# Seven-product matmul with row normalisation: products chained from bank to bank instead of combined on the vector engine

## The chip, the cores and the metric

The kernel runs on one core of one Trainium2 chip. The metric is device time in microseconds (us) of one launch. A core has five engines with a queue of instructions each, executed in the order written: TensorE (PE in the profile, its weight loads PEld), VectorE (DVE), ScalarE (ACT), GpSimd (POOL) and SyncE (SP). The last two mostly issue DMAs here. Matmuls write to PSUM, which has eight banks of 128 x 512 fp32 per core.

## The reference

```python
x = np.matmul(a, b)                                   # a, b: 2048 x 2048, fp32
rms = np.sqrt(np.mean(x ** 2, axis=-1, keepdims=True) + eps)
return (gamma * x / rms).astype(np.float32)
```

## The kernel before

The rows of a are cut into 16 row blocks of 128, the columns of b into four chunks of 512 (`CH`), the inner dimension into 16 tiles of 128, taken in 8 pairs `kp`. Matmuls take 16-bit operands (bf16 or fp16) and accumulate in fp32.

**Seven products.** Two row blocks (a *group* `g`), two column chunks (a *half* `j`: left or right 1024 columns) and the even and odd inner tiles make a 2 x 2 by 2 x 2 block product. The kernel forms its four output quarters x11, x12, x21, x22 (128 x 512 each) from seven products of eight matmuls instead of eight products. Each product has a left side, a quarter of the transposed a or a sum of two of them (`a_sums`, VectorE), and a right side, a quarter of b or a sum of two (`b_sums`, `b_sums_in_place`, VectorE), made once for all groups.

**Stages.** First, row blocks 0 to 3 (the head) are multiplied with the left columns while b arrives: TensorE transposes a, each pair `kp` is transposed through the one bank `tbank` and used at once (`stream`, `stream_in_parts`). Second, the right columns: blocks 0 and 1 plainly (`stream_right`), blocks 2 and 3, the group `PAIR`, with products 2, 5 and 1 as b arrives, and then 4, 3, 7 and 6. Third, the groups 2 to 6, each with two halves (`group_half`), and last group 7 (`last_group`).

**Order.** The schedule is written out by hand: every engine executes its instructions in the order in which the program issues them, and `hooks_of` says between which products the other work (finishing earlier rows, preparing the next a) is issued.

**In a half** (lines 582 to 626), product 2 is copied from its bank by ScalarE (L597), product 5 added to it on VectorE (L601), product 1 minus that gives t (L605). Products 4 and 3 then go on in the banks of 2 and 5 (`start=False`), are copied by ScalarE (L608, L613), squared there (L303, with the sum of squares), and added to t on VectorE (L610, L615); 7 and 6 are added on VectorE (L619, L624). So a half has six vector adds, three copies and four squares of 128 x 512. The next half uses other banks out of the seven of a rotating pool.

**Rows.** The next a is loaded as fp32 (L121, POOL), each row's norm computed on ScalarE (`row_norm`), a power of two `factor` made from it on VectorE (`row_factor`, four operations on 128 x 1), and the row scaled into fp16 (`row_apply`): on VectorE for blocks 4 and 5 (L240), on ScalarE from block 6 on (L242). A transposing DMA issued by SyncE (L195) then writes `at`. The load for the next but one group waits until the fp32 buffer is read, of which there are two. `finish` computes a row block's root (`take_rms`: reduce on VectorE L335, root on ScalarE L337), its reciprocal (L346), multiplies both halves with it and gamma (L370) and stores them (L376, SyncE).

**Last group.** The products of its right half are ordered so that row block 14 is complete early. Its last product of all, 6 of the right half, accumulates in two halves of 256 columns (L800) on banks that VectorE has filled with the rest of the sum; two squares, a root (L352), a reciprocal and the scalings follow.

## Time and profile before

| what | us |
|---|---|
| median of 3 runs | 221.31 |
| lowest, highest | 221.05, 221.69 |
| profiled execution: span from first to last instruction | 219.1 |
| first matmul of the chain's unbroken part to the end of the last matmul | 66.73 to 212.2 |
| mean granted TensorE clock | 0.994 |

The runs carry no separate time for the profiled execution: the median stands 2.2 us above its span (221.31 - 219.1), and that is taken as what lies around it.

In the profile, a row of the groups reads: line, engine, operation, output tile <- input tiles, shapes, count, then busy us, mean ns of one, and idle us before, with what ended it. A row of the order of time reads: start us, length us, what. Rows of waits read: engine, line, what it waited for, us in total, times, longest.

### The profile page before, as it was taken

To read this page: it belongs to the slowest core of one execution; us is meant where nothing else is said; L and a number is where in the kernel's file an instruction comes from. 1 tells how busy PE (TensorE), PEld (TensorE's weight loads), DVE (VectorE), ACT (ScalarE), POOL (GpSimd) and SP (SyncE) were. 2 spreads that over 40 slices of the span, in tenths; PEclk is the share of its full clock that TensorE was granted. 3 is DMA by queue.
4 is the path that set the end of the run, shared out by engine and by line. 5 is a ranking of instruction groups with operands and counts; after the bars stand their busy time and mean duration, and the time that the engine had idled before them with its cause. 6 is when DMAs were issued, how large, how long until landed. Compare 5 with 4: busy or idle time off the path is not lost.

```text
span 219.1 us, 3041 instructions
## 1 busy us (share of the span) xinstructions
PE 209.2 (95%) x1032; PEld 97.7 (45%) x1032; DVE 165.9 (76%) x326; ACT 127.0 (58%) x263; POOL 36.4 (17%) x75
## 2 busy tenths in 40 slices
PE   7799999999999999999999999999999999999970
PEld 3344544444455444444444444444444444444440
DVE  1128899999989998969696639946795759787771
ACT  2110002930599898588945996289747996334471
POOL 7554443433020002200110002000200000000040
PEclk9999999999999999999999999999999999999997
DMA  7999999999929698946799149955699259145045
GB/s 156 168 202 206 204 206 209 212 208 228 407 77 330 243 276 218 349 188 165 212 320 399 64 88 271 350 244 96 160 298 400 37 106 361 79 167 219 1 170 215
DMA packets 36720, 46.60 MB, mean 213 GB/s; under 512 B 22240, under 2 KB 26336, under 8 KB 35424
## 3 DMA queue, kind: packets, MB, share of 16 engines
q0 software_dynamic: 10608, 23.86, 44.1%
q1 hardware_dynamic: 25824, 22.29, 33.7%
q10 hardware_dynamic: 272, 0.26, 0.3%
q8 instruction: 8, 0.13, 0.2%
q14 instruction: 8, 0.07, 0.1%
HBM read 34.60 MB, written 16.78 MB: 234 GB/s over the span
## 4 chain that ended last, share of the span: by engine, by line
PE 92%; DMA 3%; ACT 1%; POOL 1%; issue 1%; DVE 0%; ACTq 0%; POOLq 0%
PE acc L285 71%; PE acc L388 16%; DMA early<-in_a_dram 3%; PE tbank L419 2%; PE tbank L168 2%; PE acc L800 1%; POOL b L102 0%; PE acc L185 0%; PE tbank L185 0%; ACT a L738 0%; DVE head_at L173 0%; ACTq L850 0%; ACT sq L803 0%; ACT rms L352 0%; POOL t_left masks.py:199 0%
## 5 line engine op out<-in xcount | busy, mean ns | idle before, releaser
L285 PE MATMUL acc<-b,s 128*128 128x512 bf16 x408 | 93.3, 379 | 0.0
L285 PEld LDWEIGHTS <-s 128*128 128x128 f16 (+1 forms) x512 | 50.0, 98 | 59.6 <-DVE s L260 0.2
L388 PE MATMUL acc<-b,head_at 128*128 128x512 bf16 x176 | 43.0, 379 | 1.2 <-DMA b<-in_b_dram 0.8
L303 ACT ACTIVATE sq<-x 128x512 bf16<-128x512 f32 x53 | 33.4, 630 | 6.9 <-DVE x L731 3.0
L370 DVE SCALAR_TENSOR_TENSOR x<-x,r,gamma_sb 128x1024 f32<-128x1024 f32 x28 | 34.9, 1282 | 0.7
L219 ACT ACTIVATE sq<-a 128x1024 bf16<-128x1024 f32 x24 | 25.3, 1054 | 3.2 <-DMA a<-in_a_dram 2.5
L388 PEld LDWEIGHTS <-head_at 128*128 128x128 bf16 x176 | 16.9, 97 | 20.4 <-issue 1.3
L242 ACT ACTIVATE head_at<-a,s 128x2048 f16<-128x2048 f32 x10 | 20.0, 1996 | 3.3 <-DVE s L229 3.3
L102 POOL DMA_DIRECT2D b<-in_b_dram x32 | 17.2, 541 | 20.6 <-DMA b<-in_b_dram 14.2
L430 ACT COPY x<-acc 128x512 f32<-128x512 f32 x5 | 2.9, 582 | 24.6 <-PE acc L388 24.6
L285 PEld LDWEIGHTS <-head_at 128*128 128x128 f16 (+1 forms) x112 | 10.9, 98 | 13.2
L285 PE MATMUL acc<-early,head_at 128*128 128x512 bf16 x64 | 14.5, 379 | 0.0
L285 PEld LDWEIGHTS <-at_even 128*128 128x128 f16 x96 | 9.4, 98 | 11.3
L285 PE MATMUL acc<-early,s 128*128 128x512 bf16 x56 | 14.2, 379 | 0.0
L260 DVE TENSOR_TENSOR s<-head_at 128x1024 f16<-128x1024 f16 (+5 forms) x22 | 13.4, 635 | 0.1
L615 DVE TENSOR_TENSOR x<-x,x 128x512 f32<-128x512 f32 x9 | 6.2, 693 | 8.8 <-ACT x L613 8.3
L127 POOL COPY pace<-x 128x1 f32<-128x1 f32 x4 | 1.7, 413 | 66.2 <-DVE x L624 64.9
L597 ACT COPY x<-acc 128x512 f32<-128x512 f32 x9 | 5.2, 573 | 11.5 <-PE acc L285 11.5
L173 DVE COPY head_at<-tbank 128x1024 bf16<-128x1024 bf16 x7 | 4.8, 692 | 8.6 <-PE tbank L168 8.5
L285 PE MATMUL acc<-t_left,s 128*128 128x512 bf16 x48 | 11.3, 379 | 0.0
L783 POOL TENSOR_SCALAR x<-x,r 128x512 f32<-128x512 f32 x1 | 2.7, 2657 | 51.2 <-DVE r L346 51.2
L276 DVE TENSOR_TENSOR b<-b 128x1024 bf16<-128x1024 bf16 x16 | 10.8, 686 | 0.2
(112 smaller groups left out, 238.0 us busy)
## 6 DMA issues: line engine op xcount, KB each, us to landing
out_dram<-x SPq DMA_DIRECT2D x29, 512.0 KB, 3.7
a<-in_a_dram POOLq DMA_DIRECT2D x10, 1024.0 KB, 9.0
b<-in_b_dram POOLq DMA_DIRECT2D x32, 256.0 KB, 10.0
a<-in_a_dram POOLq DMA_DIRECT2D x4, 512.0 KB, 9.8
early<-in_a_dram POOLq DMA_DIRECT2D x7, 256.0 KB, 10.0
gamma_sb<-in_gamma_dram POOLq DMA_DIRECT2D x2, 512.0 KB, 8.4
out_dram<-x SPq DMA_DIRECT2D x3, 256.0 KB, 2.6
out_dram<-a SPq DMA_DIRECT2D x1, 768.0 KB, 3.3
```

The lines of the kernel that those rows point to most:

```text
L102: nc.gpsimd.dma_start(out=raw[j][kp][:, t, :], in_=b[lo:lo + P, j * HALF:(j + 1) * HALF])
L173: nc.vector.tensor_copy(out=head_at[:, 2 * kp:2 * kp + 2, :, :], in_=view)
L219: nc.scalar.activation(out=junk, in_=a32[mb][:, h * HALF:(h + 1) * HALF], func=ACTF.Square, scale=2.0 ** -8, accum_out=n2[:, h:h + 1])
L242: nc.scalar.activation(out=a16[mb], in_=a32.pop(mb), func=ACTF.Copy, scale=factor.pop(mb))
L260: nc.vector.tensor_tensor(out=sum_of(g, s)[:, lo:hi, :], in0=x[:, lo:hi, :], in1=y[:, lo:hi, :], op=op)
L276: nc.vector.tensor_tensor(out=flat[:, 1:3, :], in0=flat[:, 1:3, :], in1=flat[:, 0::3, :], op=ALU.add)
L285: nc.tensor.matmul(bank, lhsT[:, kp, :], rhs, start=(start and kp == 0), stop=(kp == KP - 1), skip_group_check=not start)
L303: nc.scalar.activation(out=sq[:, 0:CH], in_=src, func=ACTF.Square, scale=inv_sqrt_n, accum_out=msq[mb][:, c:c + 1])
L370: nc.vector.scalar_tensor_tensor(out=x, in0=x, scalar=inverse_of[mb], in1=gamma_sb[:, h * HALF:(h + 1) * HALF], op0=ALU.mult, op1=ALU.mult)
L388: nc.tensor.matmul(bank, head_at[:, kt, r, :], head_rhs(c, kt), start=(kt == 0), stop=(kt == KT - 1))
L597: nc.scalar.copy(out=c, in_=one[1])
L615: nc.vector.tensor_tensor(out=t, in0=t, in1=x12, op=ALU.add)
```

## The change

The seven products take another form, in which products accumulate on one another in PSUM:

- P1 = a11 b11. Its bank is copied by ScalarE to a second bank (B1 to B2); P2 = a12 b21 then accumulates in B1, which is x11.
- P6 accumulates on the copy in B2; B2 is copied to a third bank B3. P5 accumulates in B3. P7 has a bank of its own, B7, which ScalarE copies to x21's place.
- x22 = B3 + P7's copy (VectorE). After that P3 accumulates in B3, which is x12, copied by ScalarE. P4 accumulates in B2; x21 = B2 + P7's copy (VectorE).

A half has two adds, five copies (two of them from bank to bank), and the squares run over 1024 columns (`square_half`). a needs the sums 3, 1, 2, 4 (`a_sums`), where 1 overwrites the quarter a21 and 2 is made from 1, 4 from 2; b needs `b_diff` and a chain of three in `b_rest`, the first in place.

The products of neighbouring halves are interleaved (`segment`): P6 of half n, P3 of half n-1, P2 of n, P1 of n+1, then P5, P7 and P4 of n. The hooks are replaced by this written order. All eight banks are named tiles; there is no rotating pool. The pair of the second stage takes the same form: its P1, P2, P7 while b arrives, then P6, P3, P5, P4. Its results are put together in `pair_ends`, issued in segment 0 after row block 0 is finished. Rows are scaled on VectorE for all blocks (`row_apply`). The slots of x are listed per group. In the last group the order is P6, P3 (of the half before), P2, P1, P5, then P6 (right), P3, P2 (right), P5 (right), P7, P3 (right), P7 (right), P4 and P4 (right) in two column halves.

The diff, cut (blank lines and the removed bodies of functions printed above are left out):

```diff
-    ps_t = ctx.enter_context(tc.tile_pool(name="ps_t", bufs=1, space=bass.MemoryType.PSUM))
-    ps_a = ctx.enter_context(tc.tile_pool(name="ps_a", bufs=7, space=bass.MemoryType.PSUM))
+    psum = ctx.enter_context(tc.tile_pool(name="psum", bufs=1, space=bass.MemoryType.PSUM))
...
+    tbank = psum.tile([P, CH], FP32, name="tbank")
+    acc = [psum.tile([P, CH], FP32, name=f"acc_{n}") for n in range(7)]
...
-    s_sum = {s: consts.tile([P, KP, P], FP16, name=f"s_{s}") for s in (1, 2, 5, 6, 7)}
+    s_sum = {s: consts.tile([P, KP, P], FP16, name=f"s_{s}") for s in (2, 3, 4)}
...
     def row_apply(mb):
         a16[mb] = a16_slot(mb)
-        if mb < HB + 2:
-            nc.vector.tensor_scalar_mul(out=a16[mb], in0=a32.pop(mb), scalar1=factor.pop(mb))
-        else:
-            nc.scalar.activation(out=a16[mb], in_=a32.pop(mb), func=ACTF.Copy,
-                                 scale=factor.pop(mb))
+        nc.vector.tensor_scalar_mul(out=a16[mb], in0=a32.pop(mb), scalar1=factor.pop(mb))
+    def prepare(mb):
+        row_factor(mb)
+        row_apply(mb)
+        transpose_dma(mb)
...
+    slot_of = {(r, h): r + HB * h for r in range(HB) for h in range(2)}
+    for n, slots in enumerate(((0, 4, 1, 5), (2, 6, 3, 7), (4, 5, 0, 1), (6, 7, 2, 3),
+                               (5, 1, 4, 0), (7, 3, 6, 2))):
+        for m, slot in enumerate(slots):
+            slot_of[HB + 2 * n + m % 2, m // 2] = slot
...
+    def sum_of(g, s):
+        if s == 1:
+            return quarter(g, 1, 0)
+        return s_sum[s].bitcast(BF16) if g < G0 else s_sum[s]
+    def a_sums(g, which):
+        a11, a12, a21, a22 = (quarter(g, r, c) for r in range(2) for c in range(2))
+        terms = {3: (a11, a21, ALU.subtract), 1: (a21, a22, ALU.add),
+                 2: (sum_of(g, 1), a11, ALU.subtract), 4: (a12, sum_of(g, 2), ALU.subtract)}
+        for s in which:
+            x, y, op = terms[s]
+            nc.vector.tensor_tensor(out=sum_of(g, s), in0=x, in1=y, op=op)
+    def b_quarter(j, kp, r, c):
+        return raw[j][kp][:, r, c * CH:(c + 1) * CH]
+    def b_diff(j, kp):
+        add(sums[j][:, 1, kp, :], b_quarter(j, kp, 1, 1), b_quarter(j, kp, 0, 1), ALU.subtract)
+    def b_rest(j, kp):
+        b11, t1, b21, b22 = (b_quarter(j, kp, r, c) for r in range(2) for c in range(2))
+        t2, t4 = sums[j][:, 0, kp, :], sums[j][:, 2, kp, :]
+        add(t1, t1, b11, ALU.subtract)
+        add(t2, b22, t1, ALU.subtract)
+        add(t4, b21, t2, ALU.subtract)
+    def product_matmul(g, j, m, bank, kp, start):
+        lhsT = {1: lambda: quarter(g, 0, 0), 2: lambda: quarter(g, 0, 1),
+                3: lambda: sum_of(g, 4), 4: lambda: quarter(g, 1, 1), 5: lambda: sum_of(g, 1),
+                6: lambda: sum_of(g, 2), 7: lambda: sum_of(g, 3)}[m]()
+        rhs = {1: lambda: b_quarter(j, kp, 0, 0), 2: lambda: b_quarter(j, kp, 1, 0),
+               3: lambda: b_quarter(j, kp, 1, 1), 4: lambda: sums[j][:, 2, kp, :],
+               5: lambda: b_quarter(j, kp, 0, 1), 6: lambda: sums[j][:, 0, kp, :],
+               7: lambda: sums[j][:, 1, kp, :]}[m]()
+        nc.tensor.matmul(bank, lhsT[:, kp, :], rhs, start=(start and kp == 0),
+                         stop=(kp == KP - 1), skip_group_check=not start)
+    def product(g, j, m, bank, start=True):
+        for kp in range(KP):
+            product_matmul(g, j, m, bank, kp, start)
...
+        if kp == KP - 2:
+            before.append(lambda: a_sums(PAIR, (3,)))
...
+    u2, u4, p7 = acc[4:7]
     def stream_right(kp):
         first, second = ([(g, 2 * kp + t) for g in plain] for t in range(2))
         if kp == 0:
+            for both in zip(first, second):
+                for g, kt in both:
+                    head_matmul(banks[g], *g, kt)
+            product_matmul(PAIR, 1, 1, u2, kp, True)
+            product_matmul(PAIR, 1, 2, u4, kp, True)
             return
+        product_matmul(PAIR, 1, 1, u2, kp, True)
+        for g, kt in first:
+            head_matmul(banks[g], *g, kt)
+        product_matmul(PAIR, 1, 2, u4, kp, True)
+        product_matmul(PAIR, 1, 7, p7, kp - 1, True)
+        for g, kt in second:
+            head_matmul(banks[g], *g, kt)
     for kp in range(KP):
         load_later(1)
+        b_diff(1, kp)
         stream_right(kp)
+        if kp % 2 == 0:
+            square_half(kp // 2, 0)
         if kp > 0:
+            b_rest(1, kp - 1)
         if kp == 0:
+            b_diff(0, KP - 1)
+            b_rest(0, KP - 3)
         if kp == 1:
+            b_rest(0, KP - 2)
+            b_rest(0, KP - 1)
+        if kp in (2, 3, 4):
+            a_sums(PAIR, ((1,), (2,), (4,))[kp - 2])
...
+    copy_on("A")(out=x11, in_=u2)
+    product_matmul(PAIR, 1, 7, p7, KP - 1, True)
+    add(x11, u4, x11)
+    b_rest(1, KP - 1)
+    evict(plain[:2], "DA")
     row_norm(HB)
     row_norm(HB + 1)
+    product(PAIR, 1, 6, u2, start=False)
+    nc.vector.tensor_copy(out=u4, in_=u2)
+    evict(plain[2:3], "D")
     row_factor(HB)
     row_apply(HB)
+    product(PAIR, 1, 3, acc[0])
+    product(PAIR, 1, 5, u4, start=False)
     row_factor(HB + 1)
     row_apply(HB + 1)
+    evict(plain[3:], "A")
+    turned = [transpose_half(HB, 0, tbank)]
+    for kp in range(KP):
+        product_matmul(PAIR, 1, 4, u2, kp, False)
+        if kp == 4:
+            turned.append(transpose_half(HB, 1, acc[1]))
     load_gamma(0)
     load_block(HB + 3)
+    take_transposed(HB, 0, turned[0], nc.scalar.copy)
+    turned += [transpose_half(HB + 1, h, bank) for h, bank in enumerate((tbank, acc[2]))]
+    take_transposed(HB, 1, turned[1], nc.scalar.copy)
+    for h in range(2):
+        take_transposed(HB + 1, h, turned[2 + h], nc.vector.tensor_copy)
+    a_sums(G0, (3, 1, 2))
     def pair_ends():
+        nc.scalar.copy(out=x22, in_=p7)
+        nc.scalar.copy(out=x12, in_=u4)
+        add(x21, u2, x22)
+        add(x22, x12, x22)
+        add(x12, acc[0], x12)
...
+    halves = [(g, j) for g in range(G0, NG) for j in range(2)]
+    B1, B2, B3, B7 = (acc[1], acc[0]), acc[3:5], (acc[6], acc[5]), acc[2]
+    def chunks(n):
+        g, j = halves[n]
+        return [x_chunk(2 * g + r, 2 * j + c) for r in range(2) for c in range(2)]
+    def do(n, m):
+        if n >= len(halves) or n < 0:
+            return
+        g, j = halves[n]
+        b1, b2, b3 = B1[n % 2], B2[n % 2], B3[n % 2]
+        product(g, j, m, {1: b1, 2: b1, 3: b3, 4: b2, 5: b3, 6: b2, 7: B7}[m],
+                start=m in (1, 7))
+        if m == 1:
+            nc.scalar.copy(out=b2, in_=b1)
+        elif m == 6:
+            nc.scalar.copy(out=b3, in_=b2)
+        elif m == 7:
+            nc.scalar.copy(out=chunks(n)[2], in_=B7)
+    def take(n, what, engine="A"):
+        x11, x12, x21, x22 = chunks(n)
+        if what == 11:
+            copy_on(engine)(out=x11, in_=B1[n % 2])
+        elif what == 12:
+            copy_on(engine)(out=x12, in_=B3[n % 2])
+        elif what == 22:
+            add(x22, B3[n % 2], x21)
+        else:
+            add(x21, B2[n % 2], x21)
     def load_after(g, mb):
         wait_for(at(2 * g + 3)[:, KT - 1, 0:1] if g == G0 else x_chunk(2 * g + 1, 1)[:, 0:1])
         load_block(mb)
+    def segment(n):
+        g, j = halves[n]
+        ra, rb, nxt = 2 * g, 2 * g + 1, 2 * g + 2
+        if n == 0:
+            do(n, 1)
+            take_rms(0)
+            finish(0)
+            do(n, 2)
+            pair_ends()
+            a_sums(g, (4,))
+            row_norm(nxt)
+            take_rms(1)
+            do(n, 6)
+            prepare(nxt)
+            finish(1)
+            do(n + 1, 1)
+            row_norm(nxt + 1)
+            do(n, 5)
+            do(n, 7)
+            take(n, 22)
+            take(n, 11)
+            prepare(nxt + 1)
+            do(n, 4)
+            take(n, 21)
+            square_half(rb, j)
+            return
+        if j == 1 and g + 2 < NG:
+            load_after(g, nxt + 2)
+            if g == G0:
+                wait_for(x_tile(r2, 1)[:, 0:1])
+            load_block(nxt + 3)
+        do(n, 6)
         if j == 0:
+            take_rms(ra - 1)
+            if g + 1 < NG:
+                row_norm(nxt)
+        elif g == G0:
+            square_half(r2, 1)
+            square_half(r3, 1)
+        do(n - 1, 3)
+        take(n - 1, 12)
+        square_half(halves[n - 1][0] * 2, 1 - j)
+        if j == 0:
+            a_sums(g, (4,))
+            if g == G0 + 1:
+                take_rms(r3)
+                finish(r3)
+            finish(ra - 1)
+        elif g == G0:
+            take_rms(r2)
+        do(n, 2)
+        take(n, 11)
+        if j == 0:
+            take_rms(ra - 2)
+            if g + 1 < NG:
+                prepare(nxt)
+        elif g == G0:
+            finish(r2)
         else:
+            finish(ra - 2)
+        do(n + 1, 1)
+        if j == 0 and g + 1 < NG:
+            row_norm(nxt + 1)
+        do(n, 5)
+        do(n, 7)
+        take(n, 22)
+        if j == 0 and g + 1 < NG:
+            prepare(nxt + 1)
+        if j == 1 and g + 1 < NG:
+            a_sums(g + 1, (3, 1, 2))
+        do(n, 4)
+        take(n, 21)
+        square_half(rb, j)
     def last_group():
...
+        do(n, 6)
+        take_rms(rb - 2)
+        do(n - 1, 3)
+        take(n - 1, 12)
+        square_half(ra - 2, 1)
+        a_sums(g, (4,))
+        finish(rb - 2)
+        do(n, 2)
+        take(n, 11)
+        do(n + 1, 1)
+        take_rms(ra - 2)
+        do(n, 5)
+        nc.scalar.copy(out=x22[0], in_=b3[0])
+        finish(ra - 2)
+        do(n + 1, 6)
+        do(n, 3)
+        take(n, 12)
+        square_half(ra, 0)
+        do(n + 1, 2)
+        take(n + 1, 11)
+        square_of(ra, x11[1])
+        add(xa, xa, gam_left, ALU.mult)
+        do(n + 1, 5)
+        nc.scalar.copy(out=x22[1], in_=b3[1])
+        pre_a = partial(ra, 2)
+        do(n, 7)
+        add(x22[0], x21[0], x22[0])
+        wide = a_pool.tile([P, K], FP32, name="a32")
+        chunk = [wide[:, c * CH:(c + 1) * CH] for c in range(NCH)]
+        add(chunk[1], x22[0], gam[1], ALU.mult)
+        do(n + 1, 3)
+        take(n + 1, 12)
+        square_of(ra, x12[1])
+        other = B1[0]
+        product(g, 1, 7, other)
+        halves2 = [slice(0, CH // 2), slice(CH // 2, CH)]
+        half = [bank[:, 0:CH // 2] for bank in (B1[1], b3[0])]
+        rms_a = root(msq[ra][:, 3:4], pre_a)
+        nc.scalar.copy(out=x21[1], in_=other)
+        for bank, col in zip(half, halves2):
+            add(bank, b2[1][:, col], x21[1][:, col])
         r_a = inverse(rms_a)
         left, mid = xa[:, 0:CH], xa[:, CH:]
         by_r(left, r_a)
         nc.sync.dma_start(out=rows(ra, 0, CH), in_=left)
         nc.gpsimd.tensor_scalar_mul(out=mid, in0=mid, scalar1=r_a)
         scaled_gamma(x_tile(ra, 1), x_tile(ra, 1), r_a, gamma_sb[:, HALF:])
         nc.sync.dma_start(out=rows(ra, HALF, N), in_=x_tile(ra, 1))
         nc.sync.dma_start(out=rows(ra, CH, HALF), in_=mid)
+        add(x22[1], x21[1], x22[1])
+        square_of(rb, x22[1])
+        do(n, 4)
+        add(x21[0], b2[0], x21[0])
+        square_half(rb, 0)
+        add(xb[:, 0:CH], xb[:, 0:CH], gam[0], ALU.mult)
+        add(chunk[3], x22[1], gam[3], ALU.mult)
+        pre_b = partial(rb, 2)
...
-                nc.tensor.matmul(bank, s_sum[6][:, kp, :], b_quarter(1, kp, 0, 1)[:, col],
+                nc.tensor.matmul(bank, quarter(g, 1, 1)[:, kp, :], sums[1][:, 2, kp, col],
...
-                nc.vector.tensor_scalar(out=part, in0=half_sq[:, 0:1], scalar1=pre_b,
-                                        scalar2=msq[rb][:, 2:3], op0=ALU.add, op1=ALU.add)
-        r_b = inverse_rms(half_sq[:, 1:2], part)
+                add(part, half_sq[:, 0:1], pre_b)
+        r_b = inverse(root(half_sq[:, 1:2], part))
...
+    square_half(0, 1)
+    square_half(1, 1)
+    for n in range(len(halves) - 2):
+        segment(n)
```

## The prediction

> **What bounds the kernel now.** First the page: busy time by engine and the engines' shares of the chain that ended last.

> ```profile
> span 219.1 us, 3041 instructions
> PE 209.2 (95%) x1032; PEld 97.7 (45%) x1032; DVE 165.9 (76%) x326; ACT 127.0 (58%) x263; POOL 36.4 (17%) x75
> PE 92%; DMA 3%; ACT 1%; POOL 1%; issue 1%; DVE 0%; ACTq 0%; POOLq 0%
> ```

> TensorE is the bound; no other engine is near it. Then the chain in order of time (start, length, what):

> ```profile
> 66.73 143.74 PE acc L285 x666
> 210.47 1.76 PE acc L800 x16
> ...
> 212.82 0.30 ACT rms L352
> ```

> From 66.7 us on TensorE never waits: 143.74/666 = 0.216 us per matmul, 1.73 us per product of eight. The root that opens the tail starts 0.6 us after the last matmul. So the change can gain little, and whatever makes TensorE wait lengthens the kernel one for one. A row of TensorE's waits and one of VectorE's order of time show what is already tight:

> ```profile
> PE acc L388 <- DMA b<-in_b_dram: 0.8, 1, 0.8
> 56.53 1.10 DVE L271 TENSOR_TENSOR early<-b 128x512 bf16<-128x512 bf16 x3 [0.32 <-DMA b<-in_b_dram]
> ```

> The first is TensorE's longest wait after its warm-up; the second says that the last quarter of b reaches VectorE only at 56.5. Last, the rows by shape, for prices:

> ```profile
> L260 DVE TENSOR_TENSOR s<-head_at 128x1024 f16<-128x1024 f16 x15 | 9.7, 682 | 0.0
> L601 DVE TENSOR_TENSOR x<-acc,x 128x512 f32<-128x512 f32 x9 | 6.2, 686 | 0.0
> L370 DVE SCALAR_TENSOR_TENSOR x<-x,r,gamma_sb 128x1024 f32<-128x1024 f32 x28 | 34.9, 1282 | 0.7
> L240 DVE TENSOR_SCALAR gamma_sb<-a,s 128x2048 f16<-128x2048 f32 x1 | 1.3, 1277 | 0.0
> L242 ACT ACTIVATE head_at<-a,s 128x2048 f16<-128x2048 f32 x10 | 20.0, 1996 | 3.3 <-DVE s L229 3.3
> L613 ACT COPY x<-acc 128x512 f32<-128x512 f32 x10 | 5.8, 575 | 1.7 <-issue 0.9 <-PE acc L285 0.8
> L310 ACT ACTIVATE sq<-x 128x1024 bf16<-128x1024 f32 x4 | 4.3, 1067 | 0.0
> L147 PE MATMUL acc<-sq 128*128 128x512 bf16 x8 | 3.6, 631 | 1.4 <-DVE pace L137 1.4
> ```

> and two pairs of neighbours on VectorE (start, length):

> ```profile
> 72.81 0.68 DVE L563 TENSOR_TENSOR x<-x 128x512 f32<-128x512 f32 x1
> 73.52 0.69 DVE L564 TENSOR_TENSOR x<-x,x 128x512 f32<-128x512 f32 x1
> ...
> 187.91 0.68 DVE L619 TENSOR_TENSOR x<-acc,x 128x512 f32<-128x512 f32 x1
> 188.51 0.68 DVE L260 TENSOR_TENSOR s<-head_at 128x1024 f16<-128x1024 f16 x1
> ```

> Independent operations start 0.60 apart; one that overwrites what the one before reads starts 0.71 after it.

> **The change, part by part.** "Pn" is product n. A matmul ends 0.16 us after the next could start (0.38 long against 0.216).

> *Engine totals per group of two halves.* VectorE: adds 12 to 4, sums of a 5 to 4, row scaling 0 to 2: -8x0.60 - 0.60 + 2x1.28 = -2.8 us. ScalarE: copies 6 to 10, squares 8 of 128x512 to 4 of 128x1024, row scaling out (2x2.0): about -4 us. Both were off the path: worth 0. TensorE's matmuls are as many as before: 0. Loads are issued in the same order: 0, covered by the stages before, except where named.

> *Chain copies.* P6 accumulates on a copy of P1, P5 and P3 on a copy of P6. In the loop P5, P7 and P4 of the half before (5.2 us) lie between P1 and P6, and three products between P6 and P5, against a copy of 0.58 on ScalarE: 0. ScalarE writing a bank from a bank is in no row; I take its copy from a bank (0.58), with VectorE's 0.70 into a bank as the other end; the difference stays under cover.

> *Group boundaries.* The next group opens with P6, which needs sum 2 of a. VectorE's order is fixed: the add that takes quarter 22 (needs P7's copy), sum 3, sum 1 (in place on what sum 3 reads), sum 2 (from sum 1). Only P4 (1.73) lies on TensorE between P7 and that P6. From P7's nominal end: 0.16 + copy 0.59 + 0.03, add 0.60 to the next start, 0.71, 0.71, last sum 0.68, hand-over and weight load about 0.12: 3.60; less 1.73 = **1.87 us** of waiting. Before, the sum of the opening product was made four products ahead. Behind the sums on VectorE stands the add of quarter 21, behind that ScalarE's square and P6's chain copy, there 2.5 us after P6 starts; P5 wants it at 6.9: 0 more. Groups 2-3 to 6-7 make five: **9.35**. With all starts 0.60 apart it is 1.65 each (8.2).

> *Right columns, last products of the pair.* b_diff and b_rest cost VectorE 0.34 + 0.45 + 0.45 + 0.34 = 1.57 per step (0.42 long, 0.335 apart, 0.45 if dependent) against 1.6 before; it is free again when b's last quarter lands at 56.5. Then: b_diff to 56.87, b_rest(6) to 58.1, the add on x11 to 58.7, b_rest(7) to 59.94, the eviction of acc[0] to 60.63. P6 runs 58.30 to 60.03; P3 writes acc[0] and waits to 60.65: **0.62**. If VectorE were 0.6 earlier it is 0, if b lands later it grows.

> *Opening of group 2 (segment 0).* P1 starts at 67.8 (67.2 before, +0.62). P2 follows it at once and accumulates on the very bank that is being copied: it waits 0.16 + 0.59 + 0.04 = **0.79**. P2 to 72.05, P6 to 73.78. P1 of half 1 writes acc[0], which holds the pair's P3 until the last of pair_ends. VectorE: transposed copies and three sums to 70.8, reduce, ScalarE's root 71.1, reciprocal, finish(0) 71.3 to 73.73 (2x1.20), three adds to 75.73. P1 waits 73.78 to 75.76: **1.98**. The root and the chain copy behind it reach 77.2, in time for P5 at 77.49. Half 1 of group 2 then finds its copies early (86.7 against 89.6): 0.

> *Group 3 (its P6 at 0).* ScalarE: square 0.5-1.7, copy to 2.5, root, row_norm to 5.15, take 12, square to 6.85, root of row block r3 7.05. VectorE stands from 4.45 to 7.05 for that root, then finishes r3 (to 9.67) and block 5 (12.26), and only then reduces block 4, whose root ScalarE awaits at 12.65 ahead of P1's chain copy (13.15). P6 of half 1 could start at 12.08: **1.09**. Behind it row_norm ends 15.6, P7's copy 16.2, the add that frees P3's bank 16.9; P3 could start at 14.90: **2.02**. In later groups there is no r3, and the copy is there at 8.1.

> *Row scaling on VectorE.* 1.28 for 2.0. Its transposing DMA on SP follows it, landing 4.3 after issue: the second of a group is scaled by 13.9 (P6 at 0), landed by 18.3, read at 23.9. The load on POOL that waits for its buffer is issued at 14.2 and lands in 9.0 (5.1 to 12.8), wanted at 34. Stores behind them on SP free buffers wanted half a group later. All 0; each would cost its overrun.

> *Tail.* The last products are now P7, P4 and P4 in two column halves. After P7 the seeds of 256 columns end at 22.24 (last group's P6 at 0), the reciprocal at 22.3, then on VectorE: scaling 1.20, add 0.60, add 0.68 to 24.83; ScalarE squares x of row block b 25.0-26.2 and the two column halves to 27.4; VectorE, which overwrites what that square reads, multiplies, multiplies, sums and adds from 26.1 to 27.75; root at 27.8. The last matmul ends at 24.3: 3.5 us to the root against 0.6: **2.9** (0 if these queues drain earlier, 4 if the seeds are late too).

> *Sum.* 0.62 + 0.79 + 1.98 + 9.35 + 1.09 + 2.02 + 2.9 = 18.75. The profiled span goes from 219.1 to 237.9; the median shown, 221.31, stands 2.2 above the span, and I carry that: **240.1 us**.

> *Clock.* After the 0.8 us wait above, the granted clock reads 1.00 (8 to 10 us and on). From a cold start eight matmuls took 3.60 us against 1.73, so a wait that cools TensorE costs up to 1.87. There are ten waits of 0.6 to 2.0, nearer to the 0.8: 0, at most 18.7. [...]

> *Seeds.* The kernel before already accumulates on a bank that VectorE wrote (L731, then L800's 16 matmuls in 1.76 us), at no extra instruction, so the copies get no further term. [...]

> **The rivals.** *Part of the piles drain earlier (229 to 236).* The boundary stays (8.2 to 9.4), with none to half of the rest (9.4): 221.3 + 8.2 = 229.5 at least, 234.2 with half. For it: VectorE has 2.8 us less to do per group. Against: the waits follow from order, not from load. Chance 0.16.

> *More waits (244 to 254).* In the right columns sum 1 is written in place into head_at at stride two; if that orders TensorE's next reads of head_at behind it, TensorE waits from 46.2 to 48.7, 2.4 more; or some waits cool the clock, at up to 1.87 each. No row shows a strided write beside TensorE's reads, and the page shows a clock of 9 tenths up to the tail. 243 to 252; chance 0.14.

> *The sums are hidden (219 to 223; the other side).* If sums 3, 1, 2 were done by P4's end, the boundary is 0; then the openings must vanish too. It decides if P7's end to sum 2 takes under 1.73 us; copy, add and three sums at their shortest starts are 3.3. Time 221.3 with the tail's 2.9 gone as well. Chance 0.05; faster in 0.03 of it, since nothing shortens TensorE's own work.

> **How the numbers follow.** Forecast, own range 236 to 244: 0.65. About 0.3% (0.7 us) is what this kernel's measurement can tell from no change. The range 232.5 to 247 leaves out the last rival, the lower part of the first and the upper part of the second, together under 0.2. Faster 0.03, same 0.02, slower 0.95.

> **What would show it.** In the profile after: TensorE near 209 busy in a span near 238; its waits led by "VectorE sum of a", five times some 1.9 us, about 26.0 us apart; one wait near 70 on a ScalarE copy and one near 74 on VectorE's pair add; two in group 3; ScalarE's last root 3 to 4 us after the last matmul. Wrong if sum 2 precedes P4's end, if finish(0) isn't ahead of the pair adds, or if the matmul after a wait runs slower than 0.216 apart.

## The result, and the profile after

| what | before | after |
|---|---|---|
| median, lowest to highest (4 runs each, side by side), us | 221.5 (221.05 to 221.78) | 265.87 (263.3 to 268.73) |
| ratio, 95% interval | 1 | 1.192 (1.188 to 1.196) |
| profiled execution / its span, us | not given / 219.1 | 263.89 / 262.1 |
| mean granted TensorE clock | 0.994 | 0.949 |
| first matmul of the groups to the end of the last matmul | 66.73 to 212.2 | 67.67 to 252.06 |

The ratio, and every comparison below, leaves out runs more than 1.5% above the fastest of their kernel, here 267.84 and 268.73; the other two make 263.6 us for the changed kernel. The changed kernel is 19% slower; the forecast was 240.1, with 247 as its upper end. 43.0 us of span have to be found (262.1 - 219.1), against 18.75 forecast.

The page of the changed kernel: span, busy time by engine, the granted clock over the span in 40 slices, and the shares of the chain that ended last:

```profile
span 262.1 us, 2910 instructions
PE 219.9 (84%) x1032; PEld 99.9 (38%) x1032; DVE 143.8 (55%) x278; ACT 114.4 (44%) x227; POOL 39.0 (15%) x71
PEclk9999999999997999999968999799995899999995
DMA 37%; PE 37%; DVE 13%; ACT 4%; issue 4%; POOL 2%; ACTq 0%; DVEq 0%; POOLq 0%; SPq 0%
```

Two things stand here that the forecast did not have. The chain is 37% DMA, as much as TensorE; before it was 3% against 92%. Not all of that is new waiting: 16% are loads of b in the first 56 us, a stage in which the chain of before ran through TensorE, and 16% are transposing DMAs (11 into `at_even`, 5 into `head_at`). And the clock has holes: 7 in the slice at about 80 us, then 6 and 8 near 135, 7 near 168, 5 and 8 near 200 (the last 5 is the tail). TensorE's busy time is 10.7 us more for the same 1032 matmuls.

TensorE's waits in the changed kernel (engine, output, line, what it waited for: us in total, times, longest):

```profile
PE acc L344 <- DVE s L321: 21.5, 5, 7.0
PE acc L344 <- DVE x L98: 4.7, 1, 4.7
PE acc L344 <- DVE s L229: 1.9, 1, 1.9
PE acc L344 <- ACT acc L517: 1.4, 2, 0.8
PE acc L344 <- DVE x L393: 0.6, 1, 0.6
```

These are the ten waits that were forecast, at the places that were forecast; the view has no others after the start of the right columns. (The third row names `s L229`, the first operation of `row_factor`; it stands directly behind the add of quarter 22, for which the wait was forecast.) But the first row was to be 9.35 and the second 1.98. TensorE's order of time shows which of them are longer (start, length, what, and in brackets the idle time ahead and what ended it):

```profile
78.51 5.15 PE L344 MATMUL acc<-b,at_even 128*128 128x512 bf16 x16 [4.68 <-DVE x L98]
...
100.93 1.90 PE L344 MATMUL acc<-t_left,s 128*128 128x512 bf16 x8 [1.73 <-DVE s L321]
...
135.27 3.59 PE L344 MATMUL acc<-t_left,s 128*128 128x512 bf16 x8 [7.00 <-DVE s L321]
138.66 2.40 PE L344 MATMUL acc<-b,s 128*128 128x512 bf16 x8
...
166.26 2.93 PE L344 MATMUL acc<-t_left,s 128*128 128x512 bf16 x8 [4.48 <-DVE s L321]
...
198.82 3.60 PE L344 MATMUL acc<-t_left,s 128*128 128x512 bf16 x8 [6.53 <-DVE s L321]
...
227.69 1.90 PE L344 MATMUL acc<-t_left,s 128*128 128x512 bf16 x8 [1.73 <-DVE s L321]
```

The boundaries into groups 3 and 7 wait 1.73, as worked out (1.87, less the 0.16 by which the shown wait is short, since it counts from the modelled end of the last matmul). Those into groups 4, 5 and 6 wait 7.00, 4.48 and 6.53, and after each the next eight matmuls take 2.9 to 3.6 us instead of 1.9. Only these three lie behind a group in which loads of the next a go out beside the transposing DMA: the loads of group 2 wait for that DMA in the program's text, and group 6 issues none. The chain tells what the three waited for:

```profile
119.66 13.29 DMA at_even<-head_at
133.07 0.70 DVE s L321
133.80 0.70 DVE at_even L321
134.52 0.70 DVE s L321
135.27 12.70 PE acc L344 x48
...
151.34 12.59 DMA head_at<-head_at
...
181.78 14.71 DMA at_even<-head_at
```

The transposing DMA of the group's second row block, issued at 119.66, lands 13.29 us later, and only then can VectorE make sums 3, 1 and 2, behind which the opening product stands. In the kernel before, its kind landed in 4.3 (4.4 at most); that is what the forecast used.

The sum over the trace:

| term | forecast | measured |
|---|---|---|
| pair's P3 behind an eviction | 0.62 | 0.61 + 0.16 |
| P2 behind the copy of P1 (segment 0) | 0.79 | 0.66 + 0.16 |
| P1 of half 1 behind the pair's adds | 1.98 | 4.68 + 0.16 |
| group 3: P6, then P3 | 1.09 + 2.02 | 0.79 + 1.89 + 2 x 0.16 |
| five boundaries | 9.35 | 21.47 + 5 x 0.16 |
| slow matmuls after waits | 0 (to 18.7) | 1.5 + 2.2 + 1.7 + 2.9 = 8.3 |
| tail, end of the last matmul to the end | 2.9 | 10.0 - 6.9 = 3.1 |
| sum | 18.75 | 43.1 |

The slow matmuls are the lengths above and of the eight behind them, against 1.89 per eight (3.62 per sixteen).

### The profile page after: what moved, and what is told of

Its sections match the earlier page's. It is cut to its first block, busy times and chain, and to the rows that moved or that the text cites. A ratio compares the mean times of both kernels' runs of the same rounds, so it can differ in the third digit from the quotient of the medians.

```text
span 262.1 us, 2910 instructions
## 1 busy us (share of the span) xinstructions
PE 219.9 (84%) x1032; PEld 99.9 (38%) x1032; DVE 143.8 (55%) x278; ACT 114.4 (44%) x227; POOL 39.0 (15%) x71
## 4 chain that ended last, share of the span: by engine, by line
DMA 37%; PE 37%; DVE 13%; ACT 4%; issue 4%; POOL 2%; ACTq 0%; DVEq 0%; POOLq 0%; SPq 0%
PE acc L344 37%; DMA b<-in_b_dram 16%; DMA at_even<-head_at 11%; DMA head_at<-head_at 5%; DMA early<-in_a_dram 3%; DVE x L298 3%; DMA gamma_sb<-in_gamma_dram 3%; DVE s L321 3%; DVE x L98 2%; ACT sq L221 2%; POOL b L112 1%; ACT x L521 1%; DVE head_at L321 1%; DVE early L98 1%; POOL a L131 1%
## 5 line engine op out<-in xcount | busy, mean ns | idle before, releaser
L344 PEld LDWEIGHTS <-s 128*128 128x128 f16 (+1 forms) x312 | 31.8, 103 | 68.3 <-DVE s L321 23.9
L267 ACT ACTIVATE sq<-x 128x1024 bf16<-128x1024 f32 (+1 forms) x33 | 33.6, 1018 | 47.7 <-DVE x L98 47.1
L344 PE MATMUL acc<-t_left,s 128*128 128x512 bf16 x96 | 27.1, 434 | 21.5 <-DVE s L321 21.5
L357 PE MATMUL acc<-b,head_at 128*128 128x512 bf16 x176 | 43.2, 379 | 0.1
L344 PE MATMUL acc<-b,head_at 128*128 128x512 bf16 x168 | 40.5, 379 | 0.0
L344 PE MATMUL acc<-b,at_even 128*128 128x512 bf16 x144 | 34.7, 392 | 5.3 <-DVE x L98 4.7
L98 DVE TENSOR_TENSOR x<-acc,x 128x512 f32<-128x512 f32 x24 | 16.5, 686 | 35.0 <-ACT x L521 34.9
L344 PEld LDWEIGHTS <-head_at 128*128 128x128 f16 (+1 forms) x216 | 21.1, 98 | 25.0
L344 PE MATMUL acc<-b,s 128*128 128x512 bf16 x104 | 26.9, 406 | 2.5 <-DVE s L229 1.9
L344 PE MATMUL acc<-early,s 128*128 128x512 bf16 x112 | 27.4, 379 | 0.8 <-ACT acc L517 0.8
L357 PEld LDWEIGHTS <-head_at 128*128 128x128 bf16 x176 | 16.9, 98 | 19.4 <-issue 0.7
L112 POOL DMA_DIRECT2D b<-in_b_dram x32 | 17.2, 539 | 20.4 <-DMA b<-in_b_dram 14.0
L240 DVE TENSOR_SCALAR head_at<-a,s 128x2048 f16<-128x2048 f32 x10 | 12.8, 1277 | 0.0
```

The costliest lines, as they stand in the source:

```text
L98: nc.vector.tensor_tensor(out=out, in0=in0, in1=in1, op=op)
L112: nc.gpsimd.dma_start(out=raw[j][kp][:, t, :], in_=b[lo:lo + P, j * HALF:(j + 1) * HALF])
L240: nc.vector.tensor_scalar_mul(out=a16[mb], in0=a32.pop(mb), scalar1=factor.pop(mb))
L267: nc.scalar.activation(out=sq[:, 0:src.shape[-1]], in_=src, func=ACTF.Square, scale=inv_sqrt_n, accum_out=msq[mb][:, c:c + 1])
L344: nc.tensor.matmul(bank, lhsT[:, kp, :], rhs, start=(start and kp == 0), stop=(kp == KP - 1), skip_group_check=not start)
L357: nc.tensor.matmul(bank, head_at[:, kt, r, :], head_rhs(c, kt), start=(kt == 0), stop=(kt == KT - 1))
```

## The experiments

The first theory, L: the loads cause it. In groups 3 to 5 GpSimd issues two 1 MB loads of the next a. The first waits for quarter 22 of the left half, the second besides for the fp32 buffer that the second row's scaling reads. In both kernels that is so, but the kernel before makes quarter 22 last, behind the second transposing DMA (issued at 106.04), while the change adds it ahead of the second row's `row_factor` and scaling. So the two loads now go out around that DMA, which is issued at 119.66, and it then lands late. The rows, before and then after (the copy to `pace` is GpSimd's wait):

```profile
108.54 0.18 POOL L127 COPY pace<-x 128x1 f32<-128x1 f32 x1 [19.77 <-DVE x L624]
```

```profile
117.01 0.69 DVE L98 TENSOR_TENSOR x<-acc,x 128x512 f32<-128x512 f32 x1 [1.92 <-ACT x L521]
117.83 0.18 POOL L140 COPY pace<-x 128x1 f32<-128x1 f32 x1 [23.13 <-DVE s L229]
118.36 1.35 POOL L131 DMA_DIRECT2D a<-in_a_dram  x1 [0.34 <-DVE s L231]
120.14 0.53 POOL L131 DMA_DIRECT2D a<-in_a_dram  x1 [0.42 <-issue]
```

Rivals: V, the move of the row scaling to VectorE is itself the cause; C, the waits cost mostly by cooling TensorE, and would be cheap if it were kept busy.

### Loads issued behind the transposing DMA

```diff
-        wait_for(at(2 * g + 3)[:, KT - 1, 0:1] if g == G0 else x_chunk(2 * g + 1, 1)[:, 0:1])
+        wait_for(at(2 * g + 3)[:, KT - 1, 0:1])
```

> The changed kernel, but in every group the two loads of the next but one row blocks wait for the group's second transposing DMA instead of for an add of its left half. Theory L (the loads, 2 MB issued just ahead of that transposing DMA, make it land 13 us after issue instead of 4.3): it lands in 4.3 to 5 again, TensorE's three long waits on the sums of a (7.0, 4.5, 6.5 us) fall to the 1.73 of the other two boundaries, -12.8 us, the slow matmuls behind them go, -6.8 us, and the kernel takes 244 us (241 to 248). Rival S (the transposing DMA is late for its own sake or for the stores ahead of it on SP's queue): the waits stay and the time is 258 or more.

Measured: 244.35 us (242.91 to 245.18), 1.104 of before (1.099 to 1.109), span 243.4. TensorE's waits on the sums in it:

```profile
PE acc L344 <- DVE s L321: 8.6, 5, 1.7
```

All five boundaries now wait 1.73, the worked value. The landing times of the transposing DMAs (minimum, median, maximum) in the view of their line, first in the changed kernel and then in this one:

```profile
DMA to landing us min/median/max: 4.2/4.3/14.7
```

```profile
DMA to landing us min/median/max: 4.2/4.3/4.9
```

One line of order is worth 19.2 us of 263.6. In the spans it is 18.7: 12.9 of shorter boundaries and 6.8 of slow matmuls behind them gone (2.2 + 1.7 + 2.9), less 0.8 because the 16 matmuls behind segment 0's wait were slower here (5.99). L is right as far as the changed kernel goes.

### The same edit in the kernel before, the other way round

```diff
-        wait_for(at(2 * g + 3)[:, KT - 1, 0:1] if g == G0 else x_chunk(2 * g + 1, 1)[:, 0:1])
+        wait_for(at(2 * g + 3)[:, KT - 1, 0:1] if g == G0 else x_chunk(2 * g + 1, 0)[:, 0:1])
```

> The kernel before with one edit: in groups 3 to 5 the two loads wait for quarter 21 of the left half instead of quarter 22, so they are issued some 3 to 6 us earlier, about when the second transposing DMA is. Theory L: that DMA lands 8 us or more after issue instead of 4.3, the sums of a and then TensorE wait, and the kernel gets slower by 1 to 15 us. Rival S: it lands in 4.3 and the time stays at 221.5 (220.8 to 222.2).

Measured: 230.58 us (228.87 to 231.2; one more run 235.24), 1.041 (1.035 to 1.046). In the kernel before, whose longest landing is 4.4, three transposing DMAs now land 8.9 to 11.4 after issue. VectorE waits for all three (2.8 us for the one into `head_at`, the other two below), and TensorE twice for VectorE:

```profile
DVE s L260 <- DMA at_even<-head_at: 8.7, 2, 5.2
...
PE acc L285 <- DVE s L260: 4.3, 2, 3.3
```

So the effect belongs to the order of the DMAs and not to the seven products' form. It costs less here: the landings are 3.4 to 3.7 us shorter than in the changed kernel, and of the 11.5 us that VectorE stands TensorE stands 4.3.

Put together, the issue and landing of every transposing DMA that met loads (worked out from the trace's DMA issues; us):

```
kernel                        transposing     second load      load lands   transposing lands
                              issued          issued                        (after its issue)
changed                       119.66          120.14           131.76       132.95 (13.29)
                              151.34          151.74           162.73       163.93 (12.59)
                              181.78          182.26           195.38       196.49 (14.71)
before, loads early           105.32          105.59           113.61       114.98  (9.66)
                              131.95          132.18           138.94       140.88  (8.93)
                              157.81          158.07           168.34       169.16 (11.35)
changed, loads behind         120.43          125.89           133.72       124.68  (4.25)
before                        106.04          109.59           122.43       110.32  (4.28)
```

In all six the transposing DMA lands 0.8 to 1.9 us after the load that was issued 0.2 to 0.5 us behind it, with the first load 1.3 to 2.5 us ahead of it. Where both loads are issued 3 us or more behind it, it lands in 4.3. Which of the two loads does it (the one under way, or the one that follows at once) was not separated.

### TensorE kept busy through the wait

```diff
             load_block(nxt + 3)
+        if j == 0 and G0 + 2 <= g < NG - 1:
+            for _ in range(20):
+                nc.tensor.matmul(tbank, identity_h, raw[1][0][:, 1, 0:CH], start=True, stop=True)
         do(n, 6)
```

> The changed kernel with 20 matmuls that nobody reads (4.3 us at 0.216) put into the three long waits of TensorE. Theory C (a wait of 4.5 us or more cools TensorE, and some 8 to 16 matmuls behind it run at half the rate): the waits' ends stay where they are, no matmul behind them takes more than 0.216 to the next, and the kernel gets faster by 6.8 us although TensorE does more: 257 us (254 to 260). Rival (the slow matmuls have another cause, or the waits are pushed out by the added work): 263 or more.

Measured: 271.7 us (271.59 and 271.78; two more runs 277.68 and 282.9), 1.228 (1.224 to 1.233). The gain did not come: two of the three transposing DMAs landed later still (16.40, 20.16 and 13.49 after issue, against 13.29, 12.59 and 14.71), and the filling was used up before them. The profile of this run tells C apart all the same. The filling matmuls and the product behind them, at the boundaries into groups 4 and 6:

```profile
128.90 4.48 PE L572 MATMUL tbank<-b,identity_h 128*128 128x512 bf16 x20
139.17 3.59 PE L344 MATMUL acc<-t_left,s 128*128 128x512 bf16 x8 [5.79 <-DVE s L321]
...
203.87 4.48 PE L572 MATMUL tbank<-b,identity_h 128*128 128x512 bf16 x19
209.34 1.90 PE L344 MATMUL acc<-t_left,s 128*128 128x512 bf16 x8 [0.99 <-DVE s L321]
```

Some 5 us passed without a product at the second place too, but TensorE was idle for only 0.99 of it, and its next eight matmuls are fast (1.90, against 3.59 behind 5.79 of idle time). So in this run it is idle time, not the missing data, that goes with slow matmuls; C is right in that, but cooling is 8.3 of the 43, the smaller part. Why 20 matmuls that read only what lies on the chip go with landings 3 to 8 us later in two of three places is open.

### Rows scaled on ScalarE again

```diff
-        nc.vector.tensor_scalar_mul(out=a16[mb], in0=a32.pop(mb), scalar1=factor.pop(mb))
+        if mb < HB + 2:
+            nc.vector.tensor_scalar_mul(out=a16[mb], in0=a32.pop(mb), scalar1=factor.pop(mb))
+        else:
+            nc.scalar.activation(out=a16[mb], in_=a32.pop(mb), func=ACTF.Copy,
+                                 scale=factor.pop(mb))
```

> The changed kernel with one part undone: rows of blocks 6 to 15 are scaled on ScalarE again (2.0 us) instead of VectorE (1.28). Theory L: the loads still go ahead of the second transposing DMA, which starts 2 to 3 us later; the long waits stay or grow: 260 to 272 us. Rival V (moving the scaling to VectorE is what made the transposed block late): the long waits go, 248 us or less.

Measured: 252.6 us (251.96 and 253.25; two more runs 257.02 and 257.12), 1.142 without an interval. This lies between the two theories, and neither had it. The landings are 11.08, 8.47 and 8.09, again 1.1 to 1.5 behind the second load, and the boundaries wait

```profile
PE acc L348 <- DVE s L325: 13.9, 5, 5.3
```

instead of 21.5. So V is not the cause by itself, since the collision stays, but the change with the move is some 11 us slower than without it (263.6 against 252.6): with the scaling on VectorE the loads take longer (11.0 to 13.1 us for the second, against 6.5 to 9.7). Why they do is not shown. One more row of this run is used below, two waits of about 3 us:

```profile
115.56 3.22 PE L348 MATMUL acc<-early,s 128*128 128x512 bf16 x8 [3.04 <-ACT acc L521]
...
164.13 1.90 PE L348 MATMUL acc<-t_left,s 128*128 128x512 bf16 x8 [2.78 <-DVE s L325]
```

### No transposing DMA at all

If the landing is the cause, the loads may stay as early as they are when nothing on the path is a transposing DMA. Here TensorE turns the rows of a through `tbank` in the groups, as it did for the earlier row blocks, with the eviction on VectorE.

```diff
-    def transpose_dma(mb):
-        nc.sync.dma_start_transpose(at(mb), a16[mb])
+    def turn(mb, h):
+        take_transposed(mb, h, transpose_half(mb, h, tbank), nc.vector.tensor_copy)
...
-        transpose_dma(mb)
...
         if j == 0 and g + 1 < NG:
+            turn(nxt, 0)
             prepare(nxt + 1)
...
         do(n, 4)
+        if j == 0 and g + 1 < NG:
+            turn(nxt, 1)
...
+        if j == 1 and g + 1 < NG:
+            turn(nxt + 1, 0)
         do(n - 1, 3)
+        if j == 1 and g + 1 < NG:
+            turn(nxt + 1, 1)
```

> The changed kernel with no transposing DMA: row blocks 6 to 15 are transposed by TensorE through the bank tbank (20 halves of 8 matmuls, 0.45 us each, +8.9 us) and copied out by VectorE; the loads are issued as early as in the changed kernel. Theory L (only the transposing DMA suffers from the loads ahead of it): the three long waits are 1.73 like the other two, no slow matmuls behind them, 244.3 + 8.9 = 253 us (250 to 256). Rival (early loads hurt something else too, the stores or the row work): 258 or more.

Measured: 257.32 us (256.49 to 258.72), 1.161 (1.153 to 1.170).

```profile
PE acc L343 <- DVE s L320: 8.6, 5, 1.7
PE acc L343 <- DVE x L98: 5.0, 1, 5.0
PE tbank L189 <- DVE head_at L240: 3.7, 1, 3.7
```

The boundaries are at 1.73 again, with loads as early as in the change: the loads by themselves cost TensorE nothing at the boundaries. The kernel is 4 us slower than expected, 1.3 over the theory's 256, because of the third row, a wait of the first transposes in group 3 for rows that are not scaled yet, and slow matmuls behind it (2.77 us for six). VectorE's written order makes that wait, not a load: it finishes row blocks 3 and 5 first, from 110.52 to 115.59. Against it, the change's own two waits in group 3 (0.79 and 1.89) do not occur here. The transposes themselves take 0.45 us per eight, some 9 us for 160. This version is the ground for the next three, each of which takes away one of the waits that the forecast had worked out.

### The sums ahead of the last products

Sums 3, 1 and 2 are issued before P5, P7 and P4 of the group's second half; sum 3 gets a second buffer, since P7 still reads the old one.

```diff
+        if s == 3 and g > G0 and g % 2 == 1:
+            return s_odd
...
         elif g == G0:
+            a_sums(g + 1, (3, 1, 2))
             finish(r2)
         else:
             finish(ra - 2)
+            a_sums(g + 1, (3, 1, 2))
         do(n + 1, 1)
...
-        if j == 1 and g + 1 < NG:
-            a_sums(g + 1, (3, 1, 2))
```

> The same, and sums 3, 1 and 2 of the next group's a issued before products 5, 7 and 4 of a group's second half, with a second buffer for sum 3. Theory (the waits of 1.73 us are the chain from product 7's copy over VectorE's add to sum 2): all five go, -8.6 us against the run with TensorE's transposes alone: 244.5 us (243 to 247). Rival (product 6 then waits for something else): 249 or more.

Measured: 248.6 us (248.27 to 249.94), 1.123 (1.115 to 1.130): 8.7 less than its ground, for 8.6 expected. No wait for a sum is left in it. The working of the boundary, VectorE's order against one product's length, is confirmed: it is the five waits of 1.73, and nothing behind them takes their place.

### The openings of groups 2 and 3

The adds of the pair are issued ahead of row block 0's multiplication with gamma, and row block r3 is finished at the end of the half instead of ahead of the next rows' reduction.

```diff
             take_rms(0)
-            finish(0)
             do(n, 2)
             pair_ends()
...
             do(n, 6)
+            finish(0, (1, 0))
             prepare(nxt)
...
                 take_rms(r3)
-                finish(r3)
...
         take(n, 21)
         square_half(rb, j)
+        if n == 2:
+            finish(r3)
```

> TensorE's transposes, and two edits in VectorE's order at the openings: in segment 0 the adds of pair_ends and the root of row block 1 go ahead of finishing row block 0, and row block 3 is finished at the end of group 3's first half. Theory: the wait of 4.6 us (VectorE finishing block 0, which stands for gamma, ahead of the add that frees acc[0]) falls to 0.7 and its 1.5 us of slow matmuls go, the waits of 0.8 and 1.9 us in group 3 go: -8.1 us against TensorE's transposes alone, 245 us (243 to 248). Rival (other waits take their place): 250 or more.

Measured: 249.14 us (249.05 to 249.4), 1.124 (1.116 to 1.132): 8.2 less than its ground, for 8.1 expected. The wait of 5.0 shrinks to 0.3, and with it its slow matmuls go (the next sixteen take 3.61 against 5.30): 6.5 us, where 5.4 of the 8.1 were expected. The other 2.7 were expected of the change's two waits in group 3, which the ground did not have. What goes there in their stead is the wait of 3.7 for scaled rows and its slow matmuls, against new waits of 1.4 and 2.0 for other transposes. So the theory of segment 0 is confirmed, and the agreement of the whole sum is in part luck.

### All of them, and the tail

Both sets of edits, the first eviction of the pair on ScalarE, and in the tail: the product with gamma goes to a place of its own, so that it does not wait for the square that reads the same x, and row block a's scaling goes behind it.

```diff
-    evict(plain[:2], "DA")
+    evict(plain[:2], "AD")
...
-        scaled_gamma(x_tile(ra, 1), x_tile(ra, 1), r_a, gamma_sb[:, HALF:])
...
-        add(xb[:, 0:CH], xb[:, 0:CH], gam[0], ALU.mult)
-        add(chunk[3], x22[1], gam[3], ALU.mult)
+        add(chunk[0], xb[:, 0:CH], gam[0], ALU.mult)
+        scaled_gamma(x_tile(ra, 1), x_tile(ra, 1), r_a, gamma_sb[:, HALF:])
```

> All of these edits together, the first two evictions of the pair's stage on the other engine each, and the tail's adds and squares ahead of the scaling of row block 14. If the waits that the trace shows are all that the changed form costs, it takes 253.2 - 8.6 - 8.1 - 0.3 - 2 = 234 us (232 to 237), which is the kernel before plus TensorE's transposes (8.9) plus some 4. If the form itself is slower: 239 or more.

Measured: 238.22 us (238.06 to 238.33), 1.075 (1.068 to 1.081), the best of the versions, and still slower than before. The root of the last row block, in the changed kernel and then in this one:

```profile
255.79 0.29 ACT L631 ACTIVATE rms<-n,part 128x1 f32<-128x1 f32 x1 [0.85 <-DVE part L98]
```

```profile
228.82 0.29 ACT L644 ACTIVATE rms<-n,part 128x1 f32<-128x1 f32 x1
```

The last matmuls end at 252.06 and 227.15, so the root stands 3.7 and 1.7 us behind them: the 2.0 expected of the tail edits. But the kernel ends 7.5 after the root instead of 6.3, and the last store takes 4.29 us to land instead of 3.35, so only 0.9 is kept. What remains over before, of 17.2 us of span: the transposes' 9.0, waits 4.6 with 1.0 of hand-over, the tail 2.2. The waits are the rest of the miss of 4 us: the transposes wait for their turned rows and for `factor` (2.0 and 1.4), which was not in the expectation. The time lies between the two theories (237 and 239), so whether the form itself costs something stays open; the same edits with the transposing DMAs kept have no measurement.

## Why the prediction was wrong

**What failed: the step "Row scaling on VectorE".** It set the second transposing DMA at "landing 4.3 after issue", "landed by 18.3, read at 23.9", and the load "issued at 14.2" beside it: "All 0; each would cost its overrun". Most parts were right: in groups 4 and 5 the DMA goes out 13.9 and 13.8 after P6, slow matmuls taken off (15.7 in group 3, its waits taken off), that load 0.4 to 0.5 us behind it, and the sums want it by 24. The other load, 1.3 us ahead of the DMA, was not in the working. But the 4.3 was read from transposing DMAs of before that meet no loads: there both loads go out 3 us or more behind it. In the new order they go out around it, and it lands 12.6 to 14.7 after issue, some 3 to 5 us after the sums wanted it. That is 12.1 us of waiting (21.47 + 0.8 - 9.35 = 12.9 with the hand-overs) and 6.8 of slow matmuls behind, 19.7 of the 24.3 that are missing. The step even named the overrun as the cost; it gave the landing time no upper end, though the rows of before did show one for transfers that meet (a 1 MB load took 5.1 to 12.8 us). Bounded by those, the landing would have been 4.3 to 13, up to 3.0 us past the time of reading, and with 1.87 for cooling at each of the three boundaries that have loads the range would have been open to 255 by estimate (240.1 + 3 x 4.87): beyond its end of 247, though short of the measured time.

**"Loads are issued in the same order: 0"** is where the miss began. The order on GpSimd's own queue did stay. What moved is their place against SyncE's queue: the first load waits for quarter 22 of the left half, which the new order adds ahead of the second row's scaling, and so ahead of its transposing DMA.

**Opening of group 2: 1.98 forecast, 4.84 measured.** The order was right (finish(0) ahead of the pair's adds). Unseen was that finish(0) needs gamma's left half:

```profile
73.86 2.48 DVE L298 SCALAR_TENSOR_TENSOR x<-x,r,gamma_sb 128x1024 f32<-128x1024 f32 x2 [2.33 <-DMA gamma_sb<-in_gamma_dram]
```

Its load is issued at 66.59 (64.84 before), when TensorE's transposes have read row block 4, which lies in gamma's place until then, and takes 7.2 to land:

```profile
66.59 0.53 POOL L135 DMA_DIRECT2D gamma_sb<-in_gamma_dram  x1 [0.84 <-PE acc L189]
```

Before, only one half of row block 0 was multiplied at 69.3 and the other at 75.3, so the same transfer was covered. A DMA that the moved step reads had been left out of its working.

**Clock: 0 forecast, 8.3 measured.** The choice of 0 for waits up to 2.0, its author's estimate from one wait of 0.8, holds: after every wait of 0.6 to 1.9 eight matmuls took 1.89 or 1.90. The term came in through waits that were longer than worked out. Up to 1.87 was given per wait; 1.5 to 2.9 were measured, since the slow stretch outlasts the first eight matmuls (behind the wait of 7.00 they end at 138.86, and the clock reads 0.50 until 139.68).

**What was right.** The bound and the sign were right, and so were all ten waits with what releases them. The undisturbed boundaries were right (1.73 + 0.16 for 1.87), and with them the working of VectorE's order, which the view of VectorE at the boundary into group 3 repeats start by start, three sums 0.72 apart behind the add for quarter 22:

```profile
98.13 0.69 DVE L98 TENSOR_TENSOR x<-acc,x 128x512 f32<-128x512 f32 x1 [0.53 <-ACT x L521]
98.73 0.68 DVE L321 TENSOR_TENSOR s<-head_at 128x1024 f16<-128x1024 f16 x1
99.45 0.69 DVE L321 TENSOR_TENSOR head_at<-head_at 128x1024 f16<-128x1024 f16 x1
100.18 0.69 DVE L321 TENSOR_TENSOR s<-head_at 128x1024 f16<-128x1024 f16 x1
```

So were group 3 (0.95 and 2.05 for 1.09 and 2.02), the pair (0.77 for 0.62), the copy of P1 (0.82 for 0.79) and the tail (3.1 for 2.9, the root 3.7 behind the last matmul where 3 to 4 was said). The copies ask for no matmul of their own: there are 1032 in both kernels, and a product on a copied bank takes 1.89 us per eight like any other. The copy from bank to bank, which no row had shown, costs what one to the other memory does:

```profile
L517 ACT COPY acc<-acc 128x512 f32<-128x512 f32 x12 | 6.9, 576 | 6.3 <-PE acc L344 6.3
L529 ACT COPY x<-acc 128x512 f32<-128x512 f32 x12 | 6.9, 575 | 3.4 <-PE acc L344 3.4
```

With the collision out of the way, the kernel with the loads behind ran at 244.35: the 240.1 of the forecast, gamma's 2.9, and 2.4 of slow matmuls behind that wait make 245.4.

**The rivals.** "More waits" had cooling in it, and the cooling came, though its other ground, the strided sum, did not (no wait of TensorE lies between 46.2 and 48.7); its 252 was too low, as it too took the landing for granted. "Part of the piles drain earlier" and "the sums are hidden" were wrong: no forecast wait drained, and the sums have to be moved by hand to be hidden.

## What to carry to other kernels

A DMA's landing time is a price only for the traffic it was read in (the same transposing DMA took 4.3 us, and 8.1 to 20.2 among loads): when a change moves the moment at which a buffer comes free, list what is issued within a few us of each DMA that something waits for, on all queues, and price the landing as behind the slowest of them (here it came 0.6 to 1.9 us after the second load). A wait that is worked out from an engine's written order was right to 0.1 or 0.2 us here (five kinds), and went when the instructions were moved; the waits behind a transfer were off by 2.7 us and more. Waits of TensorE of 3.0 us and more cost 1.3 to 2.9 us more than their length here, those up to 2.8 nothing.

## What the runs showed of the hardware that was not expected

- **A transposing DMA beside loads.** Alone, and with loads 3 us or more behind, it landed in 4.2 to 4.9 us. Issued 1.3 to 2.5 us after one 1 MB load and 0.2 to 0.5 ahead of another, it landed after that second load in all twelve cases of four kernels, by 0.6 to 1.9 us, which made 8.1 to 20.2 us. Its issue on SyncE took longer as well: 3.5 to 8.0 us instead of 1.7 to 3.1. Whether that is cause or effect is open:

```profile
L199 SPq DMA_TRANSPOSE at_even<-head_at x4: 1694/3557/8024, 115.3 to 181.8; - x4
```

```profile
129.44:132.85 3.41, 0.00 (x0) 0.00 (x0) 0.00 (x0) 0.00 (x0) 0.00 (x0) 1.00 1.16 173
132.85:136.26 3.41, 0.99 (x3) 0.43 (x4) 2.67 (x4) 0.35 (x1) 0.00 (x0) 0.50 0.57 233
```

```profile
111.47:114.88 3.41, 1.04 (x5) 0.39 (x4) 1.66 (x6) 2.06 (x2) 0.00 (x0) 1.00 0.96 384
159.25:162.67 3.42, 2.10 (x10) 0.78 (x8) 1.40 (x3) 0.59 (x1) 0.00 (x0) 1.00 1.09 335
162.67:166.08 3.41, 1.95 (x9) 0.90 (x10) 2.10 (x4) 1.16 (x3) 0.00 (x0) 1.00 0.29 118
```

  The wait of 3.04 leaves TensorE busy for 1.04 of 3.41 us, and half clock follows at 114.88; the wait of 2.78 falls on two stretches and leaves each above 1.9. In the changed kernel 0.50 is the only value below 1.00. A wait of 3.04 was enough, in a stretch that was not idle as a whole; what sets the clock is not shown.

- **A load's issue on GpSimd beside VectorE's row scaling.** The two loads shown at the start of the experiments differ in it: with `row_apply` running on VectorE at the same time (118.31 to 119.59), the issue took 1.35 us, and 0.53 without. It was 1.47, 1.32 and 1.33 at the other places where the two met, and 0.53 in groups 3 to 5 with the scaling on ScalarE.
